# Graph attention on one core: turning the one-hot and adding the score in one matmul, means for two blocks at once, 125-wide blocks

## Chip, cores, metric

One core of one Trainium2 chip. The metric is the device time of the kernel in microseconds (us), the median of its fast runs. The draw of inputs is the same in every run. In the profiles PE is the engine of the matmuls and PEld its loads of the stationary operand (`lhsT`, the "weights" of a load below); DVE is the vector engine, ACT the scalar engine, POOL or GpSimd the general one, SP the one that issues most transfers. The granted clock is the share of its full clock that PE had.

## The reference, cut to what matters

```python
num_nodes, in_features = x.shape            # 4096, 64
# weight: 4 heads, 64 -> 64; edge_index: 2 x 50000
x_proj[h] = x @ weight[h]
edge_scores[h] = sum(x_proj[h, src] * att_src[h]) + sum(x_proj[h, dst] * att_dst[h])
edge_scores = np.where(edge_scores > 0, edge_scores, 0.2 * edge_scores)
output[h, dst] += np.exp(edge_scores[h, i]) * x_proj[h, src]      # for every edge i
output[h, dst] /= sum(np.exp(edge_scores[h, edges_to_dst])) + 1e-8
```

## The kernel before

Stage 1, to about 128 us, sorts the edges on DVE by groups of sources and by destination. Stage 2 is a loop over blocks of `BD` = 121 destinations, 34 blocks. A block has 16 tiles (windows) of at most 128 edges. For every block it

- loads the edges' keys, broadcast to all partitions (`bc`, 1 MB), and makes one-hots from them on DVE (`oh`);
- gathers x and the two score parts of every edge by three matmuls per tile (L413, L415, L417);
- copies x (`xs`) and takes the exponentials (`ex`) on ACT; the larger of two exponentials, those of the score and of 0.2 times the score, is the weight `wv`;
- turns the one-hot of destinations by 16 transposes (L436) and two copies (`Sb`);
- multiplies x by the weights on DVE (`val`), sums weights (L459) and values (L463) over the edges by matmuls into `acc`;
- projects the sums with W (`pf`), divides (`inv`, `res`) and writes out. The projection of x follows the sum, so only 64 columns are gathered.

```python
BD = 121
...
    def gather(self, b):
        xps = self.psx.tile([P, NT, P], F32, name="xps")
        for t in range(NT):
            o = xps[:, t, 0:XC]
            T.matmul(out=o, lhsT=oh[:, 1, e], rhs=xa[:, 2 * t, :], ...)                 # L413
            T.matmul(out=o, lhsT=oh[:, 2, e], rhs=xa[:, 2 * t + 1, :], ...)             # L415
            T.matmul(out=o[:, Din:XC], lhsT=oh[:, 0, e], rhs=adb[:, b, :], ...)         # L417, 8 columns
        S.activation(out=ex, in_=xps, func=ACTF.Exp)                                    # cut
        S.copy(out=xs[:], in_=xps[:, :, 0:Din])

    def turn(self, b):
        for q in range(2):
            sp = self.pss.tile([P, NT // 2, W2], BF16, name="sp")
            for i in range(NT // 2):
                T.transpose(out=sp[:, i, :], in_=oh[:, 0, ...], identity=identb[:])     # L436
            S.copy(out=Sb[:, q * NT // 2:(q + 1) * NT // 2, :], in_=sp[:])              # L437

    def scatter(self, b):
        for t in range(NT):
            T.matmul(out=acc[:, 2 * BD:AW], lhsT=Sb[:, t, :], rhs=av(wv[:], ...), ...)  # L459, 4 columns
        for k in range(2):
            for t in range(NT):
                T.matmul(out=acc[:, k * BD:(k + 1) * BD], lhsT=val[:, t, k * P:(k + 1) * P],
                         rhs=Sb[:, t, 0:BD], ...)                                       # L463
        self.sink.take(b, acc[:])

    def run(self):
        ...
        for b in range(ND):
            self.load(b + 3)
            self.weigh(b, ...)            # wv, val
            self.gather(b + 1)
            self.turn(b + 1)
            self.onehot(b + 2)
            if b:
                self.sink.give(b - 1)     # pf, inv, res, output
            self.scatter(b)
```

## Time and profile before

| | before |
|---|---|
| runs | 316.54, 316.92, 317.27 us, and one slow one of 528.51, left out |
| median of the fast runs | 316.92 us |
| span, granted clock of the profiled run | 314.9 us, 0.822 |
| first `val` of the loop starts | 138.01 us |
| last `val` starts | 300.61 us |
| from start to start of `val`, mean of 33 | 4.93 us |

The table is read in three lengths: what comes before the first `val` (sorting, unpacking, the first block), the loop between the first and the last `val`, and the tail of 14.3 us. A change that acts in the loop shows itself as a new mean, times 32 or 33. The chain that ended last, on the page of the profile, names only PE at its end:

```profile
PE 25%; ACT 0%; DVE 0%; issue 0%
```

That is no proof that PE leads through the whole loop: the chain is followed back only over the last part of the span, 25% of it, and the timeline that the prediction quotes has DVE and PE within 1% of each other.

### The profile page before, as it was taken

How to read it: one execution, taken by the hardware profiler on the slowest of the kernel's cores; microseconds unless marked ns; L12 is line 12 of the kernel's file. 1: busy time of each engine (PE TensorE's matmuls, PEld its weight loads, DVE VectorE, ACT ScalarE, POOL GpSimd, SP SyncE). 2: the span in 40 equal slices, each digit the busy share in tenths (PEclk: the TensorE clock that was granted, in tenths of full speed). 3: DMA queues.
4: the chain of work that ended last, by engine and by line, in shares of the span. 5: the costliest groups of instructions: out<-in, count | busy, mean ns of one | idle time of the engine just before them, and what ended most of it. 6: DMA issues, size and time to landing. Idle time of an engine off the chain costs nothing. (4 is left out here: it accounts for less than half of the span.)

```text
span 314.9 us, 9697 instructions
## 1 busy us (share of the span) xinstructions
PE 207.2 (66%) x4122; PEld 202.2 (64%) x4122; DVE 275.9 (88%) x552; ACT 172.9 (55%) x324; POOL 18.6 (6%) x40
## 2 busy tenths in 40 slices
PE   0049999000000000099999999999999999999970
PEld 0027999000000000099999999999999999999970
DVE  8999999993999995479999999999999999999960
ACT  3984000000999600067777768677686767768640
POOL 6800000002000005000000000000000000000000
PEclk9999555555555555579999999999999999999996
DMA  7200000002000002991865857667575766667110
GB/s 206 46 1 0 2 0 0 1 0 67 1 0 0 0 28 51 300 395 32 284 234 224 290 191 271 216 237 251 204 276 191 258 228 253 232 227 272 56 38 21
DMA packets 13551, 43.97 MB, mean 140 GB/s; under 512 B 3308, under 2 KB 8492, under 8 KB 9148
## 3 DMA queue, kind: packets, MB, share of 16 engines
q1 hardware_dynamic: 11332, 41.92, 37.7%
q10 hardware_dynamic: 1464, 0.70, 0.8%
q0 software_dynamic: 704, 0.66, 0.8%
q8 instruction: 34, 0.56, 0.8%
q14 instruction: 17, 0.14, 0.2%
HBM read 38.22 MB, written 5.05 MB: 137 GB/s over the span
## 5 line engine op out<-in xcount | busy, mean ns | idle before, releaser
L449 DVE TENSOR_TENSOR val<-xs,wv 128x4096 bf16<-128x4096 bf16 (+1 forms) x35 | 78.0, 2231 | 4.1 <-ACT xs L423 0.7
L437 ACT COPY Sb<-sp 128x1024 bf16<-128x1024 bf16 x68 | 66.3, 1039 | 0.0
L413 PE MATMUL xps<-xa,oh 128*128 128x72 bf16 x544 | 54.1, 194 | 14.5 <-DVE oh L401 14.5
L463 PE MATMUL acc<-Sb,val 128*128 128x121 bf16 x1088 | 63.6, 217 | 0.0
L413 PEld LDWEIGHTS <-oh 128*128 128x128 bf16 x544 | 50.4, 98 | 13.9 <-DVE oh L400 13.9
L463 PEld LDWEIGHTS <-val 128*128 128x128 bf16 x1088 | 58.5, 98 | 0.1
L415 PE MATMUL xps<-xa,oh 128*128 128x72 bf16 x544 | 53.7, 195 | 0.1
L417 PE MATMUL xps<-adb,oh 128*128 128x8 bf16 x544 | 52.8, 169 | 0.0
L415 PEld LDWEIGHTS <-oh 128*128 128x128 bf16 x544 | 49.4, 96 | 1.2 <-DVE oh L401 1.1
L417 PEld LDWEIGHTS <-oh 128*128 128x128 bf16 x544 | 50.1, 97 | 0.0
L400 DVE TENSOR_SCALAR oh<-bc,pF 128x4096 bf16<-128x4096 bf16 x34 | 43.5, 1281 | 4.6 <-DMA bc<-gat_bins 4.6
L420 ACT ACTIVATE ex<-xps 128x256 bf16<-128x256 f32 x34 | 13.4, 395 | 58.3 <-PE xps L417 58.3
L188 DVE TENSOR_TENSOR sA<-sB 128x256 f32<-128x256 f32 (+2 forms) x108 | 39.6, 408 | 1.8
L250 ACT ACTIVATE junk<-kr,nb 128x512 f32<-128x512 f32 x34 | 24.5, 722 | 25.6 <-DVE kr L301 24.5
L188 DVE TENSOR_TENSOR sB<-sA 128x256 f32<-128x256 f32 (+2 forms) x100 | 36.7, 408 | 1.7
L261 PE MATMUL cnt_ps<-sgn,sel 128*128 128x17 f32 (+1 forms) x6 | 1.7, 390 | 53.1 <-ACT sgn L253 53.1
L436 PE MATMUL sp<-identb,oh 128*128 128x128 bf16 x544 | 36.5, 221 | 0.0
L261 PEld LDWEIGHTS cnt_ps<-sgn,sel 128*128 128x128 f32 x6 | 1.4, 318 | 53.2 <-issue 53.2
L423 ACT CAST xs<-xps 128x1024 bf16<-128x1024 f32 x34 | 34.1, 1003 | 0.0
L436 PEld LDWEIGHTS <-oh 128*128 128x128 bf16 x544 | 31.4, 99 | 0.0
L401 DVE TENSOR_SCALAR oh<-bc,pF 128x2048 bf16<-128x2048 bf16 x34 | 25.4, 747 | 0.0
L345 PEld LDWEIGHTS at_ps<-uv,xT 64*128 64x128 f32 x132 | 25.1, 297 | 0.4 <-issue 0.4
(116 smaller groups left out, 255.7 us busy)
## 6 DMA issues: line engine op xcount, KB each, us to landing
bc<-gat_bins SPq DMA_DIRECT2D x34, 1024.0 KB
out_dram<-res SPq DMA_DIRECT2D x33, 121.0 KB
gat_sorted<-sA SPq DMA_DIRECT2D x2, 256.0 KB
eS<-in_edge_index_dram SPq DMA_DIRECT2D x1, 390.0 KB
eD<-in_edge_index_dram ACTq DMA_DIRECT2D x1, 390.0 KB
gat_bins<-tb ACTq DMA_DIRECT2D x9, 32.0 KB
out_dram<-res SPq DMA_DIRECT2D x1, 103.0 KB
win<-gat_sorted,wi POOLq DMA_INDIRECT x5, 2.6
```

Source lines behind the costliest of these rows:

```text
L188: V.tensor_tensor(out=av(d[:], o, [2 * h, n], [1, h]), in0=av(s[:], 0, [2 * h, n], [1, h]), in1=av(s[:], h, [2 * h, n], [1, h]), op=op)
L345: T.matmul(out=ps[:, b, :], lhsT=xT[:, b * step:b * step + P], rhs=uv[:, k, :], start=(b == 0), stop=True, skip_group_check=True)
L400: V.tensor_scalar(out=oh[:, 0:2, :], in0=bc[:], scalar1=pF[:, 0:1], scalar2=None, op0=OP.is_equal)
L401: V.tensor_scalar(out=oh[:, 2, :], in0=bc[:, 1, :], scalar1=pF[:, 1:2], scalar2=None, op0=OP.is_equal)
L413: T.matmul(out=o, lhsT=oh[:, 1, e], rhs=xa[:, 2 * t, :], start=(t % 4 == 0), stop=False, skip_group_check=True)
L415: T.matmul(out=o, lhsT=oh[:, 2, e], rhs=xa[:, 2 * t + 1, :], start=False, stop=False, skip_group_check=True)
L417: T.matmul(out=o[:, Din:XC], lhsT=oh[:, 0, e], rhs=adb[:, b, :], start=False, stop=True, skip_group_check=True)
L423: S.copy(out=xs[:], in_=xps[:, :, 0:Din])
L436: T.transpose(out=sp[:, i, :], in_=oh[:, 0, t * W2:(t + 1) * W2], identity=identb[:])
L437: S.copy(out=Sb[:, q * NT // 2:(q + 1) * NT // 2, :], in_=sp[:])
L449: V.tensor_tensor(out=av(val[:], h * Dout, [Dout, n], [C, NT], [1, Din]), in0=av(xs[:], 0, [0, n], [2, NT * Din // 2], [1, 2]), in1=av(wv[ ...
L463: T.matmul(out=acc[:, k * BD:(k + 1) * BD], lhsT=val[:, t, k * P:(k + 1) * P], rhs=Sb[:, t, 0:BD], start=False, stop=(t == NT - 1), skip_g ...
```

## The change

The intent is to relieve DVE and PE, both nearly full. The matmul that adds the destination's score gets 125 identity columns behind its 8 score columns, so that it also turns the one-hot (rows of the one-hot against an identity). This removes the 16 transposes and their copies. The turned one-hot then comes out with x in one copy, in parts of 6, 6 and 4 tiles that go through two alternating PSUM buffers. Means are taken for two blocks in one DVE instruction. Blocks 125 wide make 33 of them in place of 34. The identity columns of all blocks are filled once by GpSimd during the sort. The 1e-8 of the mean comes in by a small FP32 matmul ahead of the sums. The diff, cut to its core:

```diff
-BD = 121
+BD = 125
-    eps = cst.tile([P, 1], F32)
-    V.memset(eps[:], 1e-8)
+    eps = cst.tile([1, P + 2 * H], F32)
+    V.memset(eps[:, 0:P], 1.0)
+    V.memset(eps[:, P:P + H], 1e-8)
...
-    adb = cst.tile([P, ND, 2 * H], BF16)
+    AB = 2 * H + BD
+    adb = cst.tile([P, ND, AB], BF16)
...
+        G.tensor_copy(out=adb[:, :, 2 * H:AB], in_=av(identb[:], 0, [0, ND], [1, BD]))
...
+    CH = ((0, 6), (6, 6), (12, 4))
+    S0 = Din + 2 * H
+    XW = (S0 + BD + 1) // 2 * 2
...
-        def gather(self, b):
+        def gather(self, b, c):
...
-                T.matmul(out=o[:, Din:XC], lhsT=oh[:, 0, e], rhs=adb[:, b, :], start=False, stop=True,
+                T.matmul(out=ps[:, i, Din:S0 + BD], lhsT=oh[:, 0, e], rhs=adb[:, b, :], start=False, stop=True,
...
-            S.copy(out=xs[:], in_=xps[:, :, 0:Din])
+            S.copy(out=xs[:, t0:t0 + n, 0:S0 + BD], in_=ps[:, 0:n, 0:S0 + BD])
-        def turn(self, b):          # removed whole: 16 transposes, two copies
...
-            for t in range(NT):
-                T.matmul(out=acc[:, 2 * BD:AW], lhsT=Sb[:, t, :], rhs=av(wv[:], 2 * t, [2 * NT, H]), ...)
+                T.matmul(out=self.acc[:, 2 * BD:AW], lhsT=eps[:, 0:P], rhs=self.sink.first, start=True, ...)
+                for t in range(NT):
+                    T.matmul(out=self.acc[0:BD, 2 * BD:AW], lhsT=xs[:, t, S0:S0 + BD],
+                             rhs=av(wv[:], 2 * t, [2 * NT, H]), ...)
...
-                self.gather(b + 1)
-                self.turn(b + 1)
+                self.gather(b + 1, 0)
                 self.onehot(b + 2)
                 if b:
-                    self.sink.give(b - 1)
-                self.scatter(b)
+                    self.sink.project(b - 1)
+                    if b % 2 == 0:
+                        self.sink.give(b - 2, 2)
+                self.sums(b, -1)           # eps and weights
+                self.gather(b + 1, 1)
+                self.sums(b, 0)            # values, first half
+                self.gather(b + 1, 2)
+                self.sums(b, 1)            # values, second half
...
-        win.unpack(0, nc.sync, nc.scalar)
         for b in range(3):
-            blocks.load(b)
+            blocks.load(b, (nc.sync, nc.scalar) if b == 0 else (nc.sync,))
```

In the changed kernel the lines have new numbers: gather is L433, L435, L437; `eps` L465; weight sums L468; value sums L473; `val` L454; one-hot L412 and L414.

More of the change, by code (lines that the diff above doesn't have):

```diff
@@ L110 @@
     pm8 = bits("pm8", 0, 7)
-    eps = cst.tile([P, 1], F32)
-    V.memset(eps[:], 1e-8)
+    eps = cst.tile([1, P + 2 * H], F32)
+    V.memset(eps[:, 0:P], 1.0)
+    V.memset(eps[:, P:P + H], 1e-8)
+    V.memset(eps[:, P + H:], 0.0)
     goff = cst.tile([P, 1], F32)
@@ L341, in tables @@
             S.copy(out=xT[:, 4 * q * P:4 * (q + 1) * P], in_=ps[:])
-        for k, (n, step, to) in enumerate(((NB, P, xa[:, :, Din:XC]), (ND, BD, adb[:]))):
+        for k, (n, step, to) in enumerate(((NB, P, xa[:, :, Din:XC]), (ND, BD, adb[:, :, 0:2 * H]))):
             ps = pp1.tile([P, n, H], F32, name=f"at_ps{k}")
@@ L382, in __init__, with load, onehot @@
             self.bp = pool(name="blk", bufs=2)
-            self.psx = pool(name="ps_x", bufs=1, space=PSUM)
-            self.pss = pool(name="ps_s", bufs=2, space=PSUM)
+            self.psx = pool(name="ps_x", bufs=2, space=PSUM)
             self.psa = pool(name="ps_a", bufs=1, space=PSUM)
             self.sink = sink
-            self.bc, self.oh, self.xps, self.ex, self.xs, self.wv, self.Sb, self.val = ({} for _ in range(8))
-        def load(self, b):
+            self.bc, self.oh, self.ex, self.xs, self.wv, self.val = ({} for _ in range(6))
+        def load(self, b, engs=(nc.sync,)):
             if b < ND:
                 t = self.bcp.tile([P, 2, NT * W2], BF16, name="bc")
-                nc.sync.dma_start(out=t[:], in_=dataclasses.replace(bin_dram[b], ap=[[0, P], [NT * W2, 2],
-                                                                                    [1, NT * W2]]))
+                n = NT * W2 // len(engs)
+                for i, eng in enumerate(engs):
+                    eng.dma_start(out=t[:, :, i * n:(i + 1) * n],
+                                  in_=dataclasses.replace(bin_dram[b, 0, i * NT // len(engs)],
+                                                          ap=[[0, P], [NT * W2, 2], [1, n]]))
                 self.bc[b] = t
-        def onehot(self, b):
+        def onehot(self, b, parts=1):
             if b < ND:
@@ L399, in onehot @@
                 oh = self.bp.tile([P, 3, NT * W2], BF16, name="oh")
-                V.tensor_scalar(out=oh[:, 0:2, :], in0=bc[:], scalar1=pF[:, 0:1], scalar2=None, op0=OP.is_equal)
-                V.tensor_scalar(out=oh[:, 2, :], in0=bc[:, 1, :], scalar1=pF[:, 1:2], scalar2=None, op0=OP.is_equal)
+                n = NT * W2 // parts
+                for i in range(0, NT * W2, n):
+                    V.tensor_scalar(out=oh[:, 0:2, i:i + n], in0=bc[:, :, i:i + n], scalar1=pF[:, 0:1], scalar2=None,
+                                    op0=OP.is_equal)
+                    V.tensor_scalar(out=oh[:, 2, i:i + n], in0=bc[:, 1, i:i + n], scalar1=pF[:, 1:2], scalar2=None,
+                                    op0=OP.is_equal)
                 self.oh[b] = oh
-        def gather(self, b):
+        def gather(self, b, c):
             if b >= ND:
@@ L408, in gather @@
             oh = self.oh[b]
-            xps = self.psx.tile([P, NT, P], F32, name="xps")
-            for t in range(NT):
-                o = xps[:, t, 0:XC]
+            if c == 0:
+                self.ex[b] = self.bp.tile([P, 2, H, NT, 2], BF16, name="ex")
+                self.xs[b] = self.bp.tile([P, NT, XW], BF16, name="xs")
+            ex, xs = self.ex[b], self.xs[b]
+            t0, n = CH[c]
+            ps = self.psx.tile([P, CH[0][1], 256], F32, name="ps")
+            for i in range(n):
+                t = t0 + i
@@ L412, in gather @@
                 e = slice(t * W2, (t + 1) * W2)
-                T.matmul(out=o, lhsT=oh[:, 1, e], rhs=xa[:, 2 * t, :], start=(t % 4 == 0), stop=False,
+                T.matmul(out=ps[:, i, 0:S0], lhsT=oh[:, 1, e], rhs=xa[:, 2 * t, :], start=(i % 2 == 0), stop=False,
                          skip_group_check=True)
-                T.matmul(out=o, lhsT=oh[:, 2, e], rhs=xa[:, 2 * t + 1, :], start=False, stop=False,
+                T.matmul(out=ps[:, i, 0:S0], lhsT=oh[:, 2, e], rhs=xa[:, 2 * t + 1, :], start=False, stop=False,
@@ L416, in gather @@
                          skip_group_check=True)
-                T.matmul(out=o[:, Din:XC], lhsT=oh[:, 0, e], rhs=adb[:, b, :], start=False, stop=True,
+                T.matmul(out=ps[:, i, Din:S0 + BD], lhsT=oh[:, 0, e], rhs=adb[:, b, :], start=False, stop=True,
                          skip_group_check=True)
-            ex = self.bp.tile([P, 2, H, NT, 2], BF16, name="ex")
-            S.activation(out=av(ex[:], 0, [2, NT], [2 * NT, 2 * H], [1, 2]),
-                         in_=av(xps[:], Din, [P, NT], [1, 2 * H], [0, 2]), func=ACTF.Exp)
@@ L422, in gather @@
-            xs = self.bp.tile([P, NT, Din], BF16, name="xs")
-            S.copy(out=xs[:], in_=xps[:, :, 0:Din])
-            self.ex[b], self.xs[b] = ex, xs
-        def turn(self, b):
-            if b >= ND:
-                return
-            oh = self.oh.pop(b)
-            Sb = self.bp.tile([P, NT, W2], BF16, name="Sb")
-            for q in range(2):
-                sp = self.pss.tile([P, NT // 2, W2], BF16, name="sp")
-                for i in range(NT // 2):
-                    t = q * NT // 2 + i
-                    T.transpose(out=sp[:, i, :], in_=oh[:, 0, t * W2:(t + 1) * W2], identity=identb[:])
-                S.copy(out=Sb[:, q * NT // 2:(q + 1) * NT // 2, :], in_=sp[:])
-            self.Sb[b] = Sb
+            S.activation(out=av(ex[:], 2 * t0, [2, n], [2 * NT, 2 * H], [1, 2]),
+                         in_=av(ps[:], Din, [256, n], [1, 2 * H], [0, 2]), func=ACTF.Exp)
@@ L440, in weigh @@
+            S.copy(out=xs[:, t0:t0 + n, 0:S0 + BD], in_=ps[:, 0:n, 0:S0 + BD])
+            if c == len(CH) - 1:
+                self.oh.pop(b)
         def weigh(self, b, parts=1):
-            xs, ex = self.xs.pop(b), self.ex.pop(b)
+            xs, ex = self.xs[b], self.ex.pop(b)
             wv = self.bp.tile([P, H, NT, 2], BF16, name="wv")
@@ L449, in weigh, with sums, run @@
                 V.tensor_tensor(out=av(val[:], h * Dout, [Dout, n], [C, NT], [1, Din]),
-                                in0=av(xs[:], 0, [0, n], [2, NT * Din // 2], [1, 2]),
+                                in0=av(xs[:], 0, [0, n], [XW, NT], [1, Din]),
                                 in1=av(wv[:], h * 2 * NT, [2, n * NT], [0, Din // 2], [1, 2]), op=OP.mult)
             self.val[b] = val
-        def scatter(self, b):
-            val, wv, Sb = self.val.pop(b), self.wv.pop(b), self.Sb.pop(b)
-            acc = self.psa.tile([P, AW], F32, name="acc")
-            for t in range(NT):
-                T.matmul(out=acc[:, 2 * BD:AW], lhsT=Sb[:, t, :], rhs=av(wv[:], 2 * t, [2 * NT, H]), start=(t == 0),
-                         stop=(t == NT - 1), skip_group_check=True)
-            for k in range(2):
-                for t in range(NT):
-                    T.matmul(out=acc[:, k * BD:(k + 1) * BD], lhsT=val[:, t, k * P:(k + 1) * P], rhs=Sb[:, t, 0:BD],
-                             start=False, stop=(t == NT - 1), skip_group_check=True)
-            self.sink.take(b, acc[:])
-        def run(self):
-            self.onehot(0)
-            self.gather(0)
-            self.turn(0)
+        def sums(self, b, k):
+            xs = self.xs[b]
+            if k < 0:
+                self.acc = self.psa.tile([P, AW], F32, name="acc")
+                wv = self.wv.pop(b)
+                T.matmul(out=self.acc[:, 2 * BD:AW], lhsT=eps[:, 0:P], rhs=self.sink.first, start=True, stop=False,
+                         skip_group_check=True)
+                for t in range(NT):
+                    T.matmul(out=self.acc[0:BD, 2 * BD:AW], lhsT=xs[:, t, S0:S0 + BD],
+                             rhs=av(wv[:], 2 * t, [2 * NT, H]), start=False, stop=(t == NT - 1), skip_group_check=True)
+                return
+            val = self.val[b]
+            for t in range(NT):
+                T.matmul(out=self.acc[:, k * BD:(k + 1) * BD], lhsT=val[:, t, k * P:(k + 1) * P],
+                         rhs=xs[:, t, S0:S0 + BD], start=False, stop=(t == NT - 1), skip_group_check=True)
+            if k == 1:
+                self.val.pop(b), self.xs.pop(b)
+                self.sink.take(b, self.acc[:])
+        def run(self, parts=1):
+            self.onehot(0, parts)
+            for c in range(len(CH)):
+                self.gather(0, c)
             self.onehot(1)
@@ L474, in run @@
                 self.weigh(b, 2 if b == ND - 1 else 1)
-                self.gather(b + 1)
-                self.turn(b + 1)
+                self.gather(b + 1, 0)
                 self.onehot(b + 2)
                 if b:
-                    self.sink.give(b - 1)
-                self.scatter(b)
-            self.sink.give(ND - 1)
+                    self.sink.project(b - 1)
+                    if b % 2 == 0:
+                        self.sink.give(b - 2, 2)
+                self.sums(b, -1)
@@ L483 @@
+                self.gather(b + 1, 1)
+                self.sums(b, 0)
+                self.gather(b + 1, 2)
+                self.sums(b, 1)
+            self.sink.project(ND - 1)
+            n = 2 - ND % 2
+            self.sink.give(ND - n, n)
     class Finish:
         def __init__(self, ctx):
+            self.first = eps[:, P:P + H]
             self.fp = ctx.enter_context(tc.tile_pool(name="fin", bufs=2))
             self.psf = ctx.enter_context(tc.tile_pool(name="ps_f", bufs=1, space=PSUM))
-            self.aT = {}
@@ L491, in take @@
         def take(self, b, acc):
-            aT = self.fp.tile([P, AW], F32, name="aT")
-            S.copy(out=aT[:, 0:2 * BD], in_=acc[:, 0:2 * BD])
-            S.activation(out=aT[:, 2 * BD:AW], in_=acc[:, 2 * BD:AW], func=ACTF.Identity, bias=eps[:, 0:1])
-            self.aT[b] = aT
-        def give(self, b):
-            aT = self.aT.pop(b)
-            pf = self.psf.tile([P, C], F32, name="pf")
-            for k in range(2):
-                T.matmul(out=pf[0:BD, k * P:(k + 1) * P], lhsT=aT[:, k * BD:(k + 1) * BD], rhs=Wbd[:, k, :],
-                         start=(k == 0), stop=True, skip_group_check=True)
-            inv = self.fp.tile([P, H], F32, name="inv")
-            V.reciprocal(out=inv[:], in_=aT[:, 2 * BD:AW])
-            res = self.fp.tile([P, H, Dout], F32, name="res")
-            V.tensor_tensor(out=res[0:BD], in0=av(pf[0:BD], 0, [Dout, H], [1, Dout]),
-                            in1=av(inv[0:BD], 0, [1, H], [0, Dout]), op=OP.mult)
-            n = min(BD, N - b * BD)
-            nc.sync.dma_start(out=out[b * BD:b * BD + n, :], in_=res[0:n].rearrange("p h o -> p (h o)"))
+            if b % 2 == 0:
+                self.aT = self.fp.tile([P, 2, AW], F32, name="aT")
+                self.pf = self.psf.tile([P, 2, C], F32, name="pf")
@@ new lines, in take, with project, give @@
+            S.copy(out=self.aT[:, b % 2, :], in_=acc)
+        def project(self, b):
+            for k in range(2):
+                T.matmul(out=self.pf[0:BD, b % 2, k * P:(k + 1) * P], lhsT=self.aT[:, b % 2, k * BD:(k + 1) * BD],
+                         rhs=Wbd[:, k, :], start=(b % 2 == 0 and k == 0), stop=True, skip_group_check=True)
+        def give(self, b, n):
+            inv = self.fp.tile([P, 2, H], F32, name="inv")
+            V.reciprocal(out=inv[0:BD, 0:n], in_=self.aT[0:BD, 0:n, 2 * BD:AW])
+            res = self.fp.tile([P, 2, H, Dout], F32, name="res")
+            V.tensor_tensor(out=res[0:BD, 0:n], in0=av(self.pf[0:BD], 0, [Dout, n * H], [1, Dout]),
+                            in1=av(inv[0:BD], 0, [1, n * H], [0, Dout]), op=OP.mult)
+            for i in range(n):
+                m = min(BD, N - (b + i) * BD)
+                nc.sync.dma_start(out=out[(b + i) * BD:(b + i) * BD + m, :],
+                                  in_=res[0:m, i].rearrange("p h o -> p (h o)"))
@@ L511 @@
     class Total:
         def __init__(self, total):
+            self.first = eps[:, P + H:]
             self.total = total
@@ L518, in take, with project, give @@
             V.tensor_tensor(out=self.total[:, b, :], in0=acc, in1=self.total[:, b, :], op=OP.add)
-        def give(self, b):
+        def project(self, b):
+            pass
+        def give(self, b, n):
             pass
@@ L565 @@
         for b in range(3):
-            blocks.load(b)
+            blocks.load(b, (nc.sync, nc.scalar) if b == 0 else (nc.sync,))
         for i in range(1, NI):
             win.unpack(i, nc.scalar, nc.scalar)
-        blocks.run()
+        blocks.run(2)
     order.close()
@@ L592 @@
             with ExitStack() as st:
+                V.tensor_scalar(out=total[:, :, 2 * BD:AW], in0=total[:, :, 2 * BD:AW], scalar1=1e-8, scalar2=None,
+                                op0=OP.add)
                 fin = Finish(st)
@@ L595 @@
                     fin.take(b, total[:, b, :])
-                    fin.give(b)
+                    fin.project(b)
+                    if b % 2 or b == ND - 1:
+                        fin.give(b - b % 2, b % 2 + 1)
 _INS = ['x', 'edge_index', 'weight', 'att_src', 'att_dst']
```

## The prediction

> **What bounds the kernel now.** I read the busy time by stretches first (columns: stretch, its length, then busy time and instruction count of PE, PEld, DVE, ACT and POOL, the granted clock, DMA share, GB/s).
>
> ```profile
> 20.00:40.00 20.00, 19.02 (x104) 16.41 (x103) 19.07 (x55) 7.04 (x13) 0.00 (x0) 0.80 0.00 1
> ...
> 148.00:198.00 50.00, 50.00 (x1184) 49.88 (x1181) 48.05 (x61) 36.66 (x62) 0.00 (x0) 1.00 0.66 238
> ```
>
> There are two stages. To about 128 us DVE sorts alone, and anything that stops DVE there moves the end. From 138 to 300 us the loop over 34 blocks runs, with PE and DVE both full and ACT at 73%. The timeline of one block period in the loop tells which of the two leads (start, length, engine, line):
>
> ```profile
> 192.30 2.29 DVE L449 TENSOR_TENSOR val<-xs,wv 128x4096 bf16<-128x4096 bf16 x1
> ...
> 194.51 1.28 DVE L400 TENSOR_SCALAR oh<-bc,pF 128x4096 bf16<-128x4096 bf16 x1
> ...
> 195.71 0.75 DVE L401 TENSOR_SCALAR oh<-bc,pF 128x2048 bf16<-128x2048 bf16 x1
> 196.37 0.17 DVE L504 RECIPROCAL inv<-aT 128x4 f32<-128x4 f32 x1
> 196.63 0.43 DVE L506 TENSOR_TENSOR res<-pf,inv 121x256 f32<-121x256 f32 x1
> ...
> 196.97 0.21 DVE L444 TENSOR_TENSOR wv<-ex 128x128 bf16<-128x128 bf16 x1
> ...
> 197.29 2.29 DVE L449 TENSOR_TENSOR val<-xs,wv 128x4096 bf16<-128x4096 bf16 x1
> ```
>
> DVE goes from one `val` to the next in 4.99 us with no named wait: 2.21 to the one-hot, 1.20, 0.66, 0.26, 0.34 and 0.32 between starts. Every input it needs is ready. PE takes 4.95 us when it is behind (its `pf` starts at 144.80 and again, ten blocks later, at 194.26) and 4.99 later, once it has caught up. So DVE sets the pace, and PE has only 1% to spare. The chain of work that ended last has this PE order (start, time, what):
>
> ```profile
> 263.43 0.91 PE sp L436 x16
> 264.34 0.49 PE pf L501 x4
> 264.83 0.40 PE acc L459 x16
> 265.23 1.73 PE acc L463 x32
> ```
>
> The gather of the next block fills the remaining 1.45 us. The 16 matmuls of L459, 4 columns wide, start every 25 ns: that is the time of their weight loads, since 4 columns are nearly nothing. The groups by shape give the rest (count, then busy us and mean ns):
>
> ```profile
> L437 ACT COPY Sb<-sp 128x1024 bf16<-128x1024 bf16 x68 | 66.3, 1039 | 0.0
> ...
> L423 ACT CAST xs<-xps 128x1024 bf16<-128x1024 f32 x34 | 34.1, 1003 | 0.0
> ...
> L506 DVE TENSOR_TENSOR res<-pf,inv 121x256 f32<-121x256 f32 x34 | 14.4, 425 | 3.4 <-PE pf L501 0.4
> L420 ACT ACTIVATE ex<-xps 128x256 bf16<-128x256 f32 x34 | 13.4, 395 | 58.3 <-PE xps L417 58.3
> ```
>
> **What the Trainium skill says.** (1) "TensorE: Matmul & The Clock Gate", section "Weight-path perf modes": the fast weight load is on when the number of weights is 128 and the type is not FP32. The trace agrees where it can: 128 bf16 columns load in 25 ns, 128 FP32 columns (L345, clock 0.5) in 215 ns each. No bf16 load of another width is in it. (2) "SBUF — State Buffer", section "SBUF: two separate sides": a GpSimd operation that reads SBUF and a DVE operation with two SBUF inputs exclude each other for a whole instruction. No such pair meets in the trace before, so it is untested. (3) "GPSIMD Engine Reference", section "3.1 Elementwise": 1.03 to 1.8 cycles an element at 1.2 GHz for simple loops. The trace's 128x128 FP32 tensor_scalar took 592 ns, slower still. (4) "ScalarE: Activation LUTs", section "What ACT_TABLE_LOAD costs": 186 ns + 0.833 ns an element for an ACTIVATE with immediates. `ex` at 395 ns for 256 agrees (399); the copies are nearer 150 + 0.833 n (1003 for 1024).
>
> **DVE part.** `val`, `wv` and the one-hot keep their shapes. The means now come for two blocks: `res` 512 wide is [...] 692 ns. A block without them takes 4.99 - 0.60 = 4.39 us, one with them 4.39 + 0.26 + 0.61 = 5.26; mean 4.82. With 33 blocks instead of 34, DVE alone would save some 8 us over the loop. That is the intent.
>
> **ACT part.** Copies of 6, 6 and 4 tiles by 197 columns: 150 + 0.833 n is 1.135, 1.135 and 0.806 us, 3.08 in sum against 3.08 for `xs` and the two `Sb`. Exponentials rise from 0.39 to 0.76; `aT` becomes one instruction of 0.37 in place of 0.36 + 0.27. About 4.2 us a block: not the bound.
>
> **PE part.** Sixteen transposes (0.91) go. The matmul by `adb` grows from 8 to 133 columns: [...] 58 ns against 26, so gather is 32 x 32.5 + 16 x 58 = 1.97 us against 1.45. `pf` stays at 0.49. The added FP32 eps matmul is two passes of some 107 ns: 0.21. The sums by 125 columns: 121 took 54.1 ns, so 55.7 x 32 = 1.78. The sums of weights (before L459) now load `xs` slices of **125** columns, not 128. If that loses the fast load, [...] (estimate; half the speed measured for 128) gives 54.6 ns each, 0.87 us against 0.40. PE sum: 1.97 + 0.49 + 0.21 + 0.87 + 1.78 = 5.32, less the 0.03 by which the same sum of before overshoots: **5.29 us**. With the fast load kept: 4.82.
>
> **A new loop.** The order of instructions of the changed kernel shows the last gather part of block b+1 behind the first value sums of block b, which wait for `val` of b; and `val` of b+1 needs that part. From the end of `val`: wait 0.08, 16 sums 0.89, four tiles to the start of their last matmul 0.43 (4 x 0.123 - 0.06), its run 0.22, hand-over 0.04, start of the copy 0.13, copy 0.81, hand-over 0.03, `val` 2.29: 4.92 us. A block without means (4.39 on DVE) therefore takes 4.92, one with them 5.26, and slack does not carry over: mean 5.09. The saving of pairing is lost, even with fast loads.
>
> **Loop sum.** From the start of the first `val` to that of the last, before: 138.01 to 300.61, 162.6 us. After, with 5.29 to 5.30 from PE: 32 x 5.30 = 169.6, +7.0. With fast loads: 15 x 5.26 + 17 x 4.92 = 162.5, +0.
>
> **Head and tail.** The split one-hot lets PE start 0.8 us earlier, but three copies follow one another on ACT, and ACT's last bin write waits for the second broadcast to land (its semaphore in the instruction order; some 134.3 us before): `val` of block 0 at about 138.6, +0.6. Tail, from the last `val`'s start: 2.36 + 0.05 + 0.89 + 0.2 for sums, 0.41 for `aT`, 0.75 for `pf`, 0.46 for `res` = 5.1 against 6.06: -0.9.
>
> **Sort part.** GpSimd fills `adb` with 33 x 125 identity columns, 4125 elements a partition, at about 19 us (after ACT's `identb`, 18.87). At 1.03 to 1.8 cycles that is 3.5 to 6.2 us. If the exclusion holds against the sort's two-input minima and maxima, DVE stands still for it: **+4.5 us** on the path. The `attbd` loads behind it and PE's table work come later by some 10 us, ending near 64 us, before the 70.4 us when DVE reads the counts; hidden.
>
> **Rivals.** A: slow loads and exclusion, 317.2 + 7.0 - 0.3 + 4.5 = 328. B: slow loads, no exclusion: 324. C: fast loads, exclusion: 321.5. D: fast loads, no exclusion: 317; for it speaks that no trace here has a slow 125-wide load. E: loads at FP32's measured rate, 0.83 ns a column: 1.7 us a block, PE 6.1, time about 350. F, the intent: DVE at its 4.82 mean, 308 to 310; against it stands the loop above, which uses only measured durations. All blocks fit their windows of 128 (the largest count of this draw is 123), so the slow path is not taken.
>
> **Range and chances.** I hold A and B together at about 0.6, C and D 0.3, E 0.08, and the exclusion at 0.6. The middle is 325. Low end D with a good head, high end A with a slow copy. The bar for slower is 323.6, which B straddles, so 0.52; faster needs F, 0.06.
>
> **What would show it.** Right: weight loads of the 125-wide `xs` some 50 ns apart (0.85 us for 16); `val` every 5.3 us with DVE waiting before it for ACT's copy; PE without waits; a sort stretched by the length of the `adb` copy, one DVE minimum or maximum lasting or standing 3 us or more. Wrong: 25 ns per such load, undisturbed sort, or `val` alternating 4.4 and 5.3 us, in which case the loop through the last part was not binding. A time under 312 would mean that, above 340 would mean E.

## The result, and the profile after

The changed kernel is slower: four runs of 333.40 to 334.59 us, median 333.96. The ratio to before is 1.0538 (95% interval 1.051 to 1.0566). Ratios here and below are the mean time of one kernel's fast runs over that of the other's fast runs of the same rounds, so not quite the ratio of the medians quoted.

The span grew from 314.9 to 332.2 us, by 17.3. In the three lengths:

| | before | after | difference |
|---|---|---|---|
| start of the first `val` | 138.01 | 142.15 | +4.14 |
| first `val` to start of the last | 162.60 (33 x 4.93) | 178.54 (32 x 5.58) | +15.94 |
| last `val` to the end of the last `res` | 6.06 | 5.79 | -0.27 |
| end of the last `res` to the end of the span | 8.23 | 5.72 | -2.51 |

**Sort.** The timeline of before at the time when the changed kernel fills `adb` (start, length, engine, line) shows pairs of DVE minima and maxima of 0.62 to 0.63 us:

```profile
19.52 0.62 DVE L188 TENSOR_TENSOR sA<-sB 128x192 f32<-128x192 f32 x2
20.18 0.63 DVE L188 TENSOR_TENSOR sB<-sA 128x192 f32<-128x192 f32 x2
```

The same place in the timeline of after:

```profile
19.73 3.65 POOL L314 COPY adb<-identb 128x4125 bf16<-128x4125 bf16 x1 [12.05 <-ACT identb L313]
19.81 4.05 DVE L191 TENSOR_TENSOR sA<-sB 128x192 f32<-128x192 f32 x2
...
23.90 0.63 DVE L191 TENSOR_TENSOR sB<-sA 128x192 f32<-128x192 f32 x2
```

One pair stands 4.05 us beside GpSimd's 3.65 us copy; the next is at 0.63 again. The cost is 3.42 us. The pair is shown as busy, so no wait is named: the busy time of a stretch is blind to it. In the stretches of after the instruction count tells it, 46 on DVE between 20 and 40 us where before had 55, at the same busy time:

```profile
20.00:40.00 20.00, 10.07 (x58) 7.60 (x59) 19.25 (x46) 6.70 (x12) 10.08 (x16) 0.99 0.02 3
...
148.00:198.00 50.00, 50.00 (x917) 48.78 (x916) 41.83 (x45) 34.18 (x62) 0.00 (x0) 1.00 0.56 196
```

**Loop.** The second line is the loop: PE full as before, DVE down from 48.05 to 41.83 of 50 us. The timeline of DVE after shows where it waits now:

```profile
219.88 2.29 DVE L454 TENSOR_TENSOR val<-xs,wv 128x4096 bf16<-128x4096 bf16 x1 [0.48 <-ACT xs L441]
...
225.48 2.29 DVE L454 TENSOR_TENSOR val<-xs,wv 128x4096 bf16<-128x4096 bf16 x1 [0.43 <-ACT xs L441]
...
231.07 2.29 DVE L454 TENSOR_TENSOR val<-xs,wv 128x4096 bf16<-128x4096 bf16 x1 [0.48 <-ACT xs L441]
```

A `val` starts every 5.60 and 5.59 us, with means or without, and before each DVE waits for the last copy of the block. What it waits for in the end is PE, whose order in one period is in the chain that ended last (start, time, what; the single gather matmuls are left out):

```profile
226.10 0.49 PE pf L518 x4
226.59 0.31 PE acc L465 x2
226.90 1.04 PE acc L468 x16
...
228.70 0.88 PE acc L473 x16
...
230.07 0.88 PE acc L473 x16
...
231.70 0.38 PE pf L518 x3
```

From `pf` to `pf` is 5.60 us: 0.49 + 0.31 + 1.04, then 0.76 of gather, 0.88, 0.49 of gather, 0.88, and 0.75 of gather to 231.70. No piece is a wait. The weight sums L468, 125 wide, take 65 ns each on the mean (1.04 / 16); before, 128 wide, 25 ns (0.40 / 16). That mean mixes two costs. In the records of the trace, read one by one, neighbouring sums of after end 59 ns apart (before: 26), and the first ends 150 ns behind the `eps` matmul, 0.09 us more than its own pace; in before the first ends 6 ns behind `pf`. The groups by shape give the load of the weights itself, of before

```profile
L459 PEld LDWEIGHTS <-Sb 128*128 128x128 bf16 x544 | 19.0, 96 | 0.4
```

and of after:

```profile
L468 PEld LDWEIGHTS <-xs 128*125 128x125 bf16 x528 | 33.7, 139 | 0.6
```

The mean of a load is 96 ns for 128 columns and 139 for 125. It is longer than the distance between starts because a load runs while earlier ones are still under way.

### The profile page after: what moved, and what is told of

It reads as the page before. It is cut to its first block, busy times and chain, and to the rows that moved or that the text cites. A ratio compares the mean times of both kernels' runs of the same rounds, so it can differ in the third digit from the quotient of the medians.

```text
span 332.2 us, 8424 instructions
## 1 busy us (share of the span) xinstructions
PE 223.9 (67%) x3542; PEld 215.2 (65%) x3542; DVE 273.3 (82%) x518; ACT 174.5 (53%) x349; POOL 22.2 (7%) x41
## 4 chain that ended last, share of the span: by engine, by line
PE 56%; DVE 34%; DMA 5%; issue 2%; ACT 1%; POOL 0%; DVEq 0%; SPq 0%; POOLq 0%
PE acc L473 17%; DVE sA L191 13%; DVE sB L191 11%; PE acc L468 10%; PE ps L437 9%; PE ps L433 6%; PE ps L435 5%; PE pf L518 5%; PE acc L465 3%; DMA bc<-gat_bins 1%; DMA eS<-in_edge_index_dram 1%; DVE sB L220 1%; DMA raw<-gat_sorted,wi 1%; DMA gat_bins<-tb 1%; DMA win<-gat_sorted,wi 1%
## 5 line engine op out<-in xcount | busy, mean ns | idle before, releaser
L441 ACT CAST xs<-ps 128x1182 bf16<-128x1182 f32 (+1 forms) x99 | 102.2, 1032 | 0.0
L454 DVE TENSOR_TENSOR val<-xs,wv 128x4096 bf16<-128x4096 bf16 (+1 forms) x34 | 75.7, 2229 | 15.1 <-ACT xs L441 15.1
L433 PE MATMUL ps<-xa,oh 128*128 128x72 bf16 x528 | 74.2, 198 | 13.9 <-DVE oh L412 13.6
L437 PE MATMUL ps<-adb,oh 128*128 128x133 bf16 x528 | 77.0, 226 | 0.0
L435 PE MATMUL ps<-xa,oh 128*128 128x72 bf16 x528 | 74.3, 198 | 0.0
L473 PE MATMUL acc<-xs,val 128*128 128x125 bf16 x1056 | 68.8, 217 | 0.0
L439 ACT ACTIVATE ex<-ps 128x96 bf16<-128x96 f32 (+1 forms) x99 | 24.3, 245 | 84.4 <-PE ps L437 81.4
L433 PEld LDWEIGHTS <-oh 128*128 128x128 bf16 x528 | 53.4, 102 | 12.5 <-DVE oh L412 12.5
L473 PEld LDWEIGHTS <-val 128*128 128x128 bf16 x1056 | 61.4, 97 | 0.0
L435 PEld LDWEIGHTS <-oh 128*128 128x128 bf16 x528 | 52.3, 99 | 1.9 <-DVE oh L412 1.2
L437 PEld LDWEIGHTS <-oh 128*128 128x128 bf16 x528 | 52.4, 99 | 0.0
L412 DVE TENSOR_SCALAR oh<-bc,pF 128x4096 bf16<-128x4096 bf16 (+1 forms) x34 | 42.5, 1249 | 3.5 <-DMA bc<-gat_bins 3.5
L468 PE MATMUL acc<-wv,xs 128*125 128x4 bf16 x528 | 36.5, 200 | 0.0
L468 PEld LDWEIGHTS <-xs 128*125 128x125 bf16 x528 | 33.7, 139 | 0.6
L349 PE MATMUL at_ps<-uv,xT 64*128 64x4 f32 x130 | 25.9, 336 | 0.0
L414 DVE TENSOR_SCALAR oh<-bc,pF 128x2048 bf16<-128x2048 bf16 (+1 forms) x34 | 24.9, 732 | 0.0
```

The source lines that it names most:

```text
L349: T.matmul(out=ps[:, b, :], lhsT=xT[:, b * step:b * step + P], rhs=uv[:, k, :], start=(b == 0), stop=True, skip_group_check=True)
L412: V.tensor_scalar(out=oh[:, 0:2, i:i + n], in0=bc[:, :, i:i + n], scalar1=pF[:, 0:1], scalar2=None, op0=OP.is_equal)
L414: V.tensor_scalar(out=oh[:, 2, i:i + n], in0=bc[:, 1, i:i + n], scalar1=pF[:, 1:2], scalar2=None, op0=OP.is_equal)
L433: T.matmul(out=ps[:, i, 0:S0], lhsT=oh[:, 1, e], rhs=xa[:, 2 * t, :], start=(i % 2 == 0), stop=False, skip_group_check=True)
L435: T.matmul(out=ps[:, i, 0:S0], lhsT=oh[:, 2, e], rhs=xa[:, 2 * t + 1, :], start=False, stop=False, skip_group_check=True)
L437: T.matmul(out=ps[:, i, Din:S0 + BD], lhsT=oh[:, 0, e], rhs=adb[:, b, :], start=False, stop=True, skip_group_check=True)
```

## The experiments

The theory W: a bf16 weight load is fast only where it is exactly 128 columns wide; 125 columns, a gap of three, cost the loop about half a microsecond a block. Its rivals: O, that only odd widths are slow; S, that the cost grows little by little with the columns left out, or comes from the changed source (`xs`, with rows of 198, in place of `Sb`). Beside W, each further cost found (the GpSimd copy, the FP32 `eps`, the order of the parts) has an experiment of its own. Every run was compared with before on the same chip in the same batch, where before took 316.9, 316.7 and 317.8 us.

### Loads of eight widths

The kernel before, with weight sums of falling width; the result is wrong, since rows of a block beyond the width miss edges.

```diff
-                T.matmul(out=acc[:, 2 * BD:AW], lhsT=Sb[:, t, :], rhs=...
+                w = (128, 128, 127, 127, 126, 126, 124, 124, 112, 112, 96, 96, 64, 64, 32, 32)[t]
+                T.matmul(out=acc[0:w, 2 * BD:AW], lhsT=Sb[:, t, 0:w], rhs=...
```

> The kernel before, with the 16 weight-sum matmuls of a block given stationary slices of 128, 127, 126, 124, 112, 96, 64 and 32 columns, two of each (the sums are wrong on purpose for the rows left out). Theory W (only exactly 128 columns load fast): 128 stays at some 25 ns a load, all others cost about 0.52 ns a column as the 125-wide ones of the changed kernel do (65 ns each there): 127 to 124 some 65, 112 some 58, 64 some 33 ns. Rival S (it is the row stride of 198 elements in xs, not the width): all are 25 ns or less here, where rows lie 128 apart. Rival O (only odd widths, or starts off a boundary, are slow): 127 slow, 126, 124, 112, 96 and 64 fast.

One run of 336.29 us (state unknown, one look). The groups by shape of this run, with the mean load of each width in ns after the bar:

```profile
L460 PEld LDWEIGHTS <-Sb 128*126 128x126 bf16 x68 | 6.7, 138 | 0.0
L460 PEld LDWEIGHTS <-Sb 128*124 128x124 bf16 x68 | 6.6, 138 | 0.0
L460 PEld LDWEIGHTS <-Sb 128*127 128x127 bf16 x68 | 6.6, 138 | 0.0
L460 PEld LDWEIGHTS <-Sb 128*128 128x128 bf16 x68 | 6.6, 98 | 0.4
...
L460 PEld LDWEIGHTS <-Sb 128*64 128x64 bf16 x68 | 4.7, 108 | 0.6
...
L460 PEld LDWEIGHTS <-Sb 128*32 128x32 bf16 x68 | 3.8, 94 | 0.6
```

128 columns take 98 ns and 127 take 138; 126 and 124, even, are at 138 as well. So O falls, and S falls: from 127 down the load gets shorter by 0.46 ns a column on average ((138 - 94) / 95 from 127 to 32), and only at 32 columns does it come back to what 128 cost. Leaving one column out costs 40 ns of load. What PE's stream pays is read from the records one by one: sums end 26 to 28 ns apart at 128 columns, 58 to 60 at 127 to 124, 52 at 112, 46 at 96, 33 at 64 and 27 at 32. Theory W expected this shape, from a base (65 ns at 125) that was some 6 ns too high. Where the width changes to 64 and to 32 one sum comes 123 and 109 ns after the last; no run was made for that. The records also show another access pattern for the load: [32,1,4] at 128 columns, [127,1,1] at 127, so the narrow load is written differently in the program already. The width alone does it, in the kernel before, with its own source.

### 121-wide weight sums in the kernel before

```diff
+                w = P if t == 0 else BD
-                T.matmul(out=acc[:, 2 * BD:AW], lhsT=Sb[:, t, :], rhs=...
+                T.matmul(out=acc[0:w, 2 * BD:AW], lhsT=Sb[:, t, 0:w], rhs=...
```

The first tile stays 128 wide, so that all rows that are later read are written.

> The kernel before, with 15 of 16 weight-sum loads cut from 128 to 121 columns; result correct. Theory W: 15 x some 37 ns = 0.56 us more on PE a block, PE 4.95 to 5.5 us, over DVE's 4.99, so the loop goes at PE's pace and the time rises by some 32 x 0.52 = 17 us to 334. Rivals S and O for an aligned row stride of 128: no change, or (O, 121 is odd) the same rise.

332.61 us, ratio 1.0493 (1.0467 to 1.0518); the result is correct. Of the change this run has nothing but narrow weight loads. The chain that ended last shows the 16 at 0.87 us in place of 0.40:

```profile
227.41 0.87 PE acc L460 x16
```

A `val` starts every 5.42 us in place of 4.99: the 0.47 less the 0.04 that PE had to spare. The loop grows from 162.60 to 176.65 us, the time by 15.7. In a kernel where PE has 1% to spare, seven columns cut from a weight load cost 5%.

### The changed kernel with 128 identity columns

```diff
-    AB = 2 * H + BD
+    AB = 2 * H + P
-        G.tensor_copy(out=adb[:, :, 2 * H:AB], in_=av(identb[:], 0, [0, ND], [1, BD]))
+        G.tensor_copy(out=adb[:, :, 2 * H:AB], in_=av(identb[:], 0, [0, ND], [1, P]))
-    XW = (S0 + BD + 1) // 2 * 2
+    XW = S0 + P
-                    T.matmul(out=self.acc[0:BD, 2 * BD:AW], lhsT=xs[:, t, S0:S0 + BD],
+                    T.matmul(out=self.acc[:, 2 * BD:AW], lhsT=xs[:, t, S0:XW],
```

(and the gather's matmul and copy widened likewise)

> The changed kernel with an identity of 128 columns in adb, so that the slices turned are 128 wide and the weight-sum loads too; 3 more columns a tile for PE and ACT. Theory W: PE falls from 5.60 to 5.60 - 16 x 0.039 + 0.02 = 5.0 us a block; blocks with means then take DVE's 5.26 and blocks without PE's 5.0, mean 5.13: 32 x 0.47 = 15 us less than the changed kernel, 319. Rival S: row stride is 200 still, loads stay at 65 ns, time within 1 us of 334.

322.37 us, ratio 1.0175 (1.0147 to 1.0203). The load is back at its fast rate, from the source `xs`, so S's second form falls too:

```profile
L468 PEld LDWEIGHTS <-xs 128*128 128x128 bf16 x528 | 15.8, 96 | 0.6
```

The 16 sums take 0.51 us of PE's stream in place of 1.04: they end 26 ns apart again, and the first still ends 0.11 us behind the `eps` matmul. The time is 3.4 us above the expected 319. The timeline of DVE shows what binds next:

```profile
193.88 2.29 DVE L454 TENSOR_TENSOR val<-xs,wv 128x4096 bf16<-128x4096 bf16 x1 [0.49 <-ACT xs L441]
196.43 1.29 DVE L412 TENSOR_SCALAR oh<-bc,pF 128x4096 bf16<-128x4096 bf16 x1 [0.27 <-DMA bc<-gat_bins]
...
199.51 2.29 DVE L454 TENSOR_TENSOR val<-xs,wv 128x4096 bf16<-128x4096 bf16 x1
```

The `val` before these starts at 188.97, so 4.91 us for a block without means, with the 0.49 us wait for the last copy in it: this is the loop through the last gather part, which the prediction put at 4.92. The next, with means, takes 5.63 where 5.26 was expected: it waits 0.27 us for its load. Such waits for `bc`, nine in the loop and 3.0 us in all, are what the expectation left out.

### The identity filled by ACT

```diff
-        G.tensor_copy(out=adb[:, :, 2 * H:AB], in_=av(identb[:], 0, [0, ND], [1, BD]))
+        S.copy(out=adb[:, :, 2 * H:AB], in_=av(identb[:], 0, [0, ND], [1, BD]))
```

> The changed kernel with the identity columns of adb filled by ACT instead of GpSimd. Theory: the exclusion between GpSimd and DVE costs 3.4 us (two DVE minima took 4.05 us beside the 3.65 us copy instead of 0.63), so the sort and the whole are 3.4 us shorter, 330.5; ACT's 3.5 us copy delays the table work, hidden. Rival (the sort's delay comes from elsewhere, such as the later loads of the tables): no change, 334.

330.71 us, ratio 1.0434 (1.0409 to 1.0459), as expected. The same copy, as long and at the same moment, no longer touches DVE (timeline of this run):

```profile
19.74 3.66 ACT L314 COPY adb<-identb 128x4125 bf16<-128x4125 bf16 x1
19.82 0.63 DVE L191 TENSOR_TENSOR sA<-sB 128x192 f32<-128x192 f32 x2
```

The first `val` comes at 138.65 in place of 142.15, 3.50 us earlier. The exclusion is between GpSimd and DVE, and it is the whole cost of the fill.

### A bf16 eps

```diff
-    eps = cst.tile([1, P + 2 * H], F32)
+    eps = cst.tile([1, P + 2 * H], BF16)
```

> The changed kernel with the ones, 1e-8 and zeros of the eps matmul in BF16 instead of FP32 (result correct within rounding). If PE bounds the loop at 5.60 us, of which the FP32 eps matmul is 0.31, and a BF16 one with 128 columns takes some 0.03, a block takes 5.32 us and the time falls by 32 x 0.28 = 9 us to 325. If the loop through the last part bounded it, no change: 334.

328.89 us, ratio 1.0405 (1.0359 to 1.045). The chain in this run:

```profile
229.31 0.10 PE acc L465
229.42 1.04 PE acc L468 x16
```

The matmul's place in PE's stream shrank from 0.31 to 0.10 us, not to the 0.03 expected, and the period from 5.60 to 5.40 us. The sign is right; the size missed because the bf16 matmul still took 0.10. The 1.04 behind it stayed: the 0.09 us before the first weight sum does not come from FP32. No run takes the matmul out altogether. That the period follows PE by the full 0.2 us shows once more that PE sets it.

### Another order of the parts

```diff
                 self.gather(b + 1, 1)
+                self.gather(b + 1, 2)
                 self.sums(b, 0)
-                self.gather(b + 1, 2)
                 self.sums(b, 1)
```

> The changed kernel with the last gather part of the next block put before the first value sums instead of behind them, so that ACT's copy of it no longer waits for val. If PE bounds the loop (theory), its work is the same: 334 within 1 us. If the loop val, sums, gather, copy, val bounds it (rival), a block falls towards DVE's 4.82 and the time by up to 20 us.

335.16 us, ratio 1.0576 (1.0531 to 1.062). `val` still starts every 5.60 us; the runs of the two kernels overlap (334.1 to 336.2, and 333.4 to 334.6). This opens the loop through the last gather part and gains nothing: in the changed kernel as it stands, PE is the bound and not the loop. The rival "the loop costs the time" is refuted for this kernel. With the narrow loads mended, it has to be asked again.

### Three mends together

128 columns, the fill by ACT and the bf16 `eps` (the three edits above):

> 128-wide loads, adb filled by ACT and BF16 eps together. PE 5.60 - 0.62 - 0.28 + 0.02 = 4.72 us. Theory: with the wide loads alone the loop was already at 4.91 (the loop through the last part) and 5.26 plus a wait for the broadcast load, so the eps term is worth nothing more here: w128 less 3.4 us, 319. Rival (PE still sets the pace at 5.0 there): 319 less 32 x 0.28 = 310.

319.49 us, ratio 1.0124 (1.006 to 1.0189), as expected. Starts of `val` alternate 4.91 and 5.29 to 5.87 us. The 322.37 of 128 columns less the 3.25 that the fill by ACT brought are 319.1 already, so the bf16 `eps` is worth nothing that shows within the runs' spread (318.79 to 322.60): PE is no longer the bound.

### Three mends and the other order

> As three, with the last gather part before the value sums. Theory: blocks without means fall from 4.91 to DVE's 4.39, those with means stay at 5.26 plus the wait for the broadcast; 16 x 0.52 = 8 us less than three, 311; PE at 4.72 allows it on average. Under 308 would mean that the waits for the broadcast vanish too, no gain that the loop was no loop.

318.17 us, ratio 1.0035 (0.9993 to 1.0078): a miss of 7 us. The blocks without means did fall to 4.41 us, as the theory of the loop says, from 216.96 to 221.37 for example. But DVE then waits elsewhere, in the timeline of DVE:

```profile
221.37 2.29 DVE L454 TENSOR_TENSOR val<-xs,wv 128x4096 bf16<-128x4096 bf16 x1
225.03 1.29 DVE L412 TENSOR_SCALAR oh<-bc,pF 128x4096 bf16<-128x4096 bf16 x1 [1.37 <-DMA bc<-gat_bins]
```

In the loop there are 12 such waits, 9.0 us in all, which take back the 8 us expected. (A 13th, of 4.3 us, lies before the first `val`; before has one of 3.7 us there too.) The timeline of SP, which issues the transfers, shows why the loads are late:

```profile
216.75 0.68 SPq L529 DMA_DIRECT2D out_dram<-res  x2
217.47 0.83 SPq L401 DMA_DIRECT2D bc<-gat_bins  x2
227.90 0.68 SPq L529 DMA_DIRECT2D out_dram<-res  x2
228.62 0.84 SPq L401 DMA_DIRECT2D bc<-gat_bins  x2
```

Outputs and loads share one queue and are issued in pairs, every second block, the loads only after the outputs. In program order these loads stand behind outputs that wait for the means of two blocks. That the order in the queue holds them, and not their buffer, is read from this and not tried by itself.

### A fourth buffer for the loads

```diff
-            self.bcp = pool(name="bc", bufs=3)
+            self.bcp = pool(name="bc", bufs=4)
-                self.load(b + 3)
+                self.load(b + 4)
-        for b in range(3):
+        for b in range(4):
```

Once on the three mends in the old order, and once with the new order:

> As three, with four broadcast buffers and loads issued four blocks ahead. Theory: the waits for the broadcast in blocks with means (5.26 became 5.3 to 5.6 in three) go, blocks alternate 4.91 and 5.26 by the loop through the last part and by DVE, mean 5.09: about 32 x 0.08 = 3 us less than three, 316 to 317.

> As three_reorder, with four broadcast buffers and loads issued four blocks ahead. In three_reorder 13 waits for the broadcast load took back what the broken loop gave. Theory: with the loads early enough blocks take 4.41 and 5.26, mean 4.83, DVE without waits: from 139.7 as start of the first val, 32 x 4.83 + 5.1 + 6 = 305.5 us span, time 308. Rival (the loads are limited by the DMA engines' rate, not by when they are issued): the waits stay and the time stays near 318.

The old order took 315.81 us, ratio 0.9927 (0.9897 to 0.9958); the new order 308.93 us, ratio 0.9724 (0.9708 to 0.974). Both are as expected. In the old order `val` alternates 4.91 and 5.28 us, the waits for `bc` gone: the loop alone. In the new order the timeline of DVE has

```profile
221.63 2.29 DVE L454 TENSOR_TENSOR val<-xs,wv 128x4096 bf16<-128x4096 bf16 x1
...
226.08 2.29 DVE L454 TENSOR_TENSOR val<-xs,wv 128x4096 bf16<-128x4096 bf16 x1 [0.17 <-ACT xs L441]
...
231.36 2.29 DVE L454 TENSOR_TENSOR val<-xs,wv 128x4096 bf16<-128x4096 bf16 x1
```

4.45 and 5.28 us, mean 4.87. PE's period is 4.87 too (`pf` at 226.86 and 231.73), and from 150 to 290 us it is busy for all 140.0 us: both are full again. The 4.72 that was expected of PE was too low, since the wide loads saved 0.53 and not 0.62, and the bf16 `eps` 0.20 and not 0.28. The loop through the last part was worth 6.9 us, once the loads were no longer in its place. The buffer removes the waits; whether a second queue for the outputs would do the same was not run.

### Two further runs on the best version

The bin writes of the later windows issued by SP rather than ACT, so that ACT does not stand before its first copy:

```diff
-            win.unpack(i, nc.scalar, nc.scalar)
+            win.unpack(i, nc.sync, nc.sync)
```

> As three_reorder_pre, with the bin writes of the later blocks issued by the sync engine's queue, so that ACT is not held by them (to 138.3 us in the changed kernel) when the first gather part is ready. Expected: the first val 0.5 to 1 us earlier, time 0.5 to 1 us less than three_reorder_pre. Rival: the sync queue's own later loads then come late and DVE waits in the first blocks, no gain or a loss.

307.03 us, ratio 0.9651 (0.9633 to 0.9669), the best of all. The gain is 1.9 us where at most 1 was expected; the first `val` comes 0.36 us earlier (138.68 for 139.04) and the last `res` starts 0.35 us earlier (298.65 for 299.00), so the rest lies behind it, in the writing of the last output. Why that got shorter was not followed.

Means taken block by block in place of two at a time, without the edit above (cut):

```diff
-                    if b % 2 == 0:
-                        self.sink.give(b - 2, 2)
+                    self.sink.give(b - 1, 1)
```

> As three_reorder_pre, with the means block by block again. If DVE sets the pace there, a block takes 4.99 us instead of 4.83 and the time rises by 32 x 0.16 = 5 us: this is what the pairing of the means is worth once nothing else binds. If something else binds (DMA, PE at 4.72), less.

310.62 us, ratio 0.9777 (0.9761 to 0.9793). The loop grows by 3.5 us (158.7 for 155.2; `val` every 4.99), but the time by only 1.7: from the end of the last `res` to the end of the span it is 5.7 us in place of 7.5. Why was not followed; the last of 33 blocks is alone in both kernels. Pairing is worth less than the 5 us expected.

| kernel | median us | ratio to before |
|---|---|---|
| after | 333.96 | 1.0538 |
| 121-wide loads in before | 332.61 | 1.0493 |
| after, other order | 335.16 | 1.0576 |
| after, fill by ACT | 330.71 | 1.0434 |
| after, bf16 eps | 328.89 | 1.0405 |
| after, 128 columns | 322.37 | 1.0175 |
| three mends | 319.49 | 1.0124 |
| three mends, other order | 318.17 | 1.0035 |
| three mends, four buffers | 315.81 | 0.9927 |
| three mends, other order, four buffers | 308.93 | 0.9724 |
| the same, means one by one | 310.62 | 0.9777 |
| the same with pairs, bin writes by SP | 307.03 | 0.9651 |

With a bar of 2%, the last three are faster than before; three mends, with either order of the parts, and three mends with four buffers are the same; 128 columns alone is unclear; the rest are slower.

## Why the prediction was right or wrong

The direction and the mechanism were right, the size was not: 325 was the middle, A with a slow copy the high end (some 330 by the prediction's own figures: 328, and 6.2 in place of 4.5 us for the copy), and 333.96 was measured. Rival A (slow loads and the exclusion) is what happened; it was put at 328, and even as the known case it was 6 us short. By the steps:

| step | predicted | measured |
|---|---|---|
| gather | 1.97 | 2.00 |
| `pf` | 0.49 | 0.49 |
| eps matmul | 0.21 | 0.31, and 0.09 until the first weight sum |
| weight sums, 125 wide | 0.87 | 0.95 (16 x 59 ns) |
| value sums | 1.78 | 1.76 |
| correction | -0.03 | none |
| PE's period | 5.29 | 5.60 |
| loop | +7.0 | +15.94 |
| `adb` fill against the sort | +4.5 | +3.42 |
| rest of the head | +0.6 | +0.72 |
| last `val` to last `res` | -0.9 | -0.27 |
| writing of the last output | not in the sum | -2.51 |

(Times in us; the first seven rows are for one block.)

- **The step that failed** is the PE sum, 5.29 us where 5.60 was measured, by two mis-sized terms. The larger is the `eps` matmul, "two passes of some 107 ns: 0.21". It took 0.31, and the first weight sum then came another 0.09 late: 0.40, or 0.19 too little. That 0.09 is there in all kernels with the matmul that were read for it (after, bf16 `eps`, 128 columns, three mends, the best order), and not in before or with 121-wide loads, where the sums follow `pf`. The second is the slow weight load, an estimate that "gives 54.6 ns each, 0.87 us against 0.40": 59 ns each and 0.95, or 0.08 too little. (Half the speed measured for 128, as it says, would be 49 ns; measured is 1 / 2.3.) The correction of 0.03 and small differences make up the 0.31 us a block. Times 32 this is 9.9 us; the loop missed by 8.9, since the sum had counted with 5.30 and the first period was still 4.91. The other costs held: `res` for two blocks took 692 ns as forecast, an `adb` matmul some 59 ns for 58.
- **Luck** made the total look better. The loop's 8.9 us were offset by a sort stretched 1.1 us less than said and by a last output written 2.5 us faster, for which the sum had no term; the tail gave back 0.6.
- Both terms are a matter of a sum in which nothing was slack. Where an engine is the only bound, an error of 6% in its period is one of 9 us in the end, and the high end took only a slow copy into account and no error of the PE sum. E (loads at FP32's rate) was the only rival above; between A and E there was nothing.
- **The condition for the fast load** was rightly read: 127, 126 and 124 columns are slow, 128 is fast, in the kernel before as in the changed one. The chance of 0.3 for C and D, which pulled the middle from 328 to 325, was for a rival that does not exist.
- **The exclusion** was right in kind: a 3.65 us copy stopped a DVE pair of 0.63 us for 3.42 us, and the same copy on ACT costs nothing. The size was near the low end of what was said.
- **The signs named** came: `val` evenly spaced, DVE waiting for ACT's copy before each, PE without waits, one stretched minimum in the sort. Only the distances were larger: 59 ns for some 50 between loads, 5.6 us for 5.3 between `val`.
- **The new loop** (4.92 for a block without means) did not show in the changed kernel, since PE was slower still; once the loads were mended it was there with 4.91 us. It was not the bound of this kernel, but it was the next.
- **The tail**: the writing of the last output shrank by 2.51 us. No run was made for it, and its cause stays open.
- F, the intent (308 to 310), is where the change arrives after five further edits, at 308.93.

## What to carry to other kernels

In this kernel bf16 slices of weights with few columns against them should be exactly 128 columns wide, even when some columns are not needed: the three identity columns saved cost 11.6 us (333.96 to 322.37). A GpSimd copy that reads SBUF doesn't belong beside two-input DVE work that sets the end, and ACT could do it for nothing. When a change moves little or backwards, mend the bound that the trace shows, then look for the next one: here four limits stood one behind the other (weight loads, the last gather part, loads behind outputs in one queue, and at last the work of DVE and PE themselves), and removing the second brought 1.3 us before the third was gone and 6.9 after.

## What the Trainium skill lacked or had wrong

- "TensorE: Matmul & The Clock Gate", section "Weight-path perf modes": the condition (128 weights, not FP32) is confirmed, and the runs add how sharp it is: 127 columns 138 ns, 128 columns 98 ns. The page puts the gain at about 2 times; in PE's stream it was 59 ns for 125 columns against 26 for 128, 2.3 times. Its section on LDWEIGHTS gives columns / 1.2 ns, which would be 104 ns for 125; the stream measured 59, and a load by itself lasts 139.
- "SBUF — State Buffer", section "SBUF: two separate sides": the exclusion is confirmed, with 4.05 us for a DVE pair of 0.63 beside a GpSimd copy of 3.65. The page doesn't say that a profile shows the blocked instruction as busy, with no wait named.
- "GPSIMD Engine Reference", section "3.1 Elementwise": the bf16 copy of 4125 elements a partition took 3.65 us, 1.06 cycles an element at the page's 1.2 GHz, so near the low end of its range. The section has no figure for a plain copy.
- "ScalarE: Activation LUTs", section "What ACT_TABLE_LOAD costs": the 186 ns that it gives are for an ACTIVATE, and the exponentials agree (255 ns for 96 elements, 226 for 64, leave 175 and 173). It has no figure for a copy (COPY or CAST in the trace), whose fixed part is smaller (813 ns for 788 elements and 1141 for 1182, at 0.833 ns an element, leave 157 and 156).
- None of the pages gives a figure for what one matmul of a single row costs in the midst of others of 128 rows: with 4 columns, FP32 took 0.31 us and bf16 0.10, and in both cases the first matmul behind it came 0.09 us late.
